# Whole tiles for half tiles, and sums of squared keys issued later, in the preparation of an RWKV-7 and attention encoder layer

## The chip, the cores and the metric

The kernel runs on one core of a Trainium2 chip. Times are device microseconds of one execution; the figure for a kernel is the median of several timed executions. The profile is of one further execution, taken by the hardware profiler, and its times run from the start of the span.

## The reference

One encoder layer over 512 tokens of width 1024, in float32. A normalised input is projected; the columns feed an RWKV-7 branch (8 heads of 64, two directions), a differential attention branch, and two gates. Cut to what the change touches:

```
k, r, v   = slices of centred_shift(rmsnorm(x) @ w_in)
kk        = k * k_k, per head divided by its norm: kk / sqrt(sum(kk * kk))
decay     = exp(-exp(w_log)),  a = sigmoid(...)             # per token and direction
k_dir     = k * (1 + (a - 1) * k_a)
# scan over the tokens, one per direction, state of 64 x 64 per head:
sa        = state @ (-kk_t)
state     = state * w_t + sa (x) (kk_t * a_t) + v_t (x) k_t
y_t       = state @ r_t
```

The kernel replaces the scan by eight chunks of 64 tokens. For each chunk it needs products of r, kk, k and a with running products of the decay, and the 64 x 64 matrices between them.

## The kernel before

**Stages.** The program first normalises and projects (lines 297 to 330), then comes the *preparation* (335 to 552), in which this change lies; after it the program reads back what the preparation wrote, inverts the triangular blocks on VectorE (`diag_blocks`) between the steps of the attention, and runs the chunks one after another, then the output projections and the feed-forward part.

**Precision.** Each dense product is three matmuls (`mm3`, lines 245 to 247): a high and a low half of the weights (`whi`, `wlo`, made by ScalarE in line 131 and VectorE in line 135 from `raw`) against a high and a low half of the activations. One projection of 128 columns is 24 matmuls.

**First half of the preparation.** `proj_in` makes the four key tiles: projections `in4` to `in7`, each emptied from PSUM by VectorE into the single buffer `un` (line 369) and shifted into `k` by ScalarE (370) and VectorE (371, 372). ScalarE squares each key tile into `ksq` (406). `key_sums(p)` (line 398) lets TensorE add these squares per head into the PSUM tile `nrm`: four small matmuls of 8 columns (two records each). It is called two projections later, and the last two are placed among the matmuls of the next dense product, `pp`, four tiles in each of two halves (`pp00`, `pp10` and on: the first digit is the tile, the second the half). `issue_after(last_mm.ins)` fixes the place of the sums on TensorE behind the last dense matmul that had been issued. ScalarE empties `pp` into the tile `pps` (432). When all sums are there, ScalarE and VectorE make the reciprocal norm, and TensorE turns it (`kin`, line 442).

**The loop.** For four head pairs p and two directions d (eight turns) the program makes: `sg`, `th` (ScalarE), the running sum `en` (VectorE, 478 or 480), its exponentials `ep` and `en` (ScalarE), `kd` (492), `ae` (494), the tile `bkt` by two products (500 and 499), and the tiles `ga`. A `ga` tile holds four chunks of 512 columns; there are two for each turn, h = 0 and 1. Columns 448 to 511 are r times `ep` (503), 385 to 447 are minus kk times the shifted `ep` (505 or 508), and column 384 is a copy on ScalarE (506 or 509). TensorE then multiplies `bkt` with these 128 columns (`aps`, 517), VectorE masks the result into columns 0 to 255 of the same tile (519), TensorE turns `bkt` (`xps`, 522) and ScalarE puts that into columns 256 to 383 (523). SyncE writes the tile to DRAM (`gad`, 525) and its diagonal blocks to another tensor (`md`, 528). The tag `ga` has four buffers of four chunks each, which `lr`, `pps` and these tiles take in turn; a buffer is written again when all that read it, DMAs too, have finished.

**Order.** Each engine works through its instructions in order. Within a stage a scheduler sets that order from the data and the places given; a changed instruction therefore moves others around it. TensorE's dense matmuls of later tiles (`in`, `da`) fill the time between the small ones.

Of the kernel before, what the change touches and what calls it, by code (L numbers as in the profile page):

```python
# [10 lines left out]
F32 = mybir.dt.float32  # L11
F32R = mybir.dt.float32r
AF = mybir.ActivationFunctionType
ALU = mybir.AluOpType
AX = mybir.AxisListType

P = 128
# [3 lines left out]
NCH = T // C  # L21
# [133 lines left out]
def tile_hybrid_encoder(ctx, tc, xT, wts, par, cst_a, cst_p, lor, lqk, nfin, out, dbg=None):  # L155
    nc = tc.nc
# [178 lines left out]
    pp = pool("prep", side="right")  # L335
    cp = pp.tile([P, CP["bk"]], F32, name="cp")
    nc.sync.dma_start(cp, cst_p[:, 0:CP["bk"]])
    lr = pp.tile([P, 2, 512], F32, tag="ga", name="lr", bufs=4)
    nc.sync.dma_start(lr, lor[:, 0:2, :])


# [53 lines left out]
    def key_sums(p):  # L395
        with tc.issue_after(last_mm.ins):
            for tt in range(4):
                nc.tensor.matmul(nrm[:, tt, :], sqs[p][:, tokens(tt)], cp[:, CP["selk"] + 8 * p:CP["selk"] + 8 * p + 8], start=(p == 0 and tt == 0), stop=(p == 3 and tt == 3))

    kt = []  # L400
    for p in range(4):
        k_ = tmp("k", f"k{p}", bufs=4)
        proj_in(4 + p, k_)
        kt.append(k_)
        sq = tmp(("sg", "th")[p % 2], f"ksq{p}", bufs=2)
        nc.scalar.activation(sq, k_, AF.Square, scale=par_col("kk", p))
        sqs[p] = sq
        if p > 1:
            key_sums(p - 2)
    for kind in range(2):  # L410
        for d in range(2):
            rows, other = lrows(kind, d)
# [7 lines left out]
    pTh, pTl = W.next("pT")  # L420
    for h in range(2):
        wh, wl = W.next("pp", h)
        pps = pp.tile([P, 4, 512], F32, tag="ga", name=f"pps{h}", bufs=4)
        for tt in range(4):
            ps = psd.tile([P, T], F32, tag="d", name=f"pp{tt}{h}") if tt % 2 == 0 else psm.tile([P, T], F32, tag="m", name=f"pp{tt}{h}")
            for k in range(2):
                tk = slice(k * T + tt * P, k * T + (tt + 1) * P)
                wk = slice(k * 512, (k + 1) * 512)
                last_mm = mm3(ps, pTh[:, tk], pTl[:, tk], wh[:, wk], wl[:, wk], k == 0, k == 1)
            if h == 0 and tt in (0, 2):  # L430
                key_sums(2 + tt // 2)
            nc.scalar.activation(pps[:, tt, :], ps, AF.Copy)
        nc.sync.dma_start(ppd[:, :, h * 512:(h + 1) * 512].rearrange("a q f -> q a f"), pps)

# [11 lines left out]
    for p in range(4):  # L446
# [17 lines left out]
        for d in range(2):  # L464
# [29 lines left out]
            nc.vector.scalar_tensor_tensor(ae, th, 1.0, en, ALU.add, ALU.mult)  # L494
            aec, kdc, rc = chunks(ae), chunks(kd), chunks(r_)
            bkt = pp.tile([P, NCH, P], F32, tag="bk", name=f"bk{p}{d}", bufs=2)
            ga = [pp.tile([P, 4, 512], F32, tag="ga", name=f"ga{p}{d}{h}", bufs=4) for h in range(2)]
            rv_ = slice(None, None, 1 if d == 0 else -1)
            nc.vector.scalar_tensor_tensor(bkt[:, :, 0:C][:, :, rv_], aec, 0.5, kkc, ALU.mult, ALU.mult)
            nc.vector.tensor_tensor(bkt[:, :, C:P], kdc, enc, ALU.mult)  # L500
            for h in range(2):
                hs = slice(4 * h, 4 * h + 4)
                nc.vector.tensor_tensor(ga[h][:, :, 448:512], rc[:, hs, :], epc[:, hs, :], ALU.mult)
                if d == 0:
                    nc.vector.scalar_tensor_tensor(ga[h][:, :, 385:448], kkc[:, hs, 1:], -1.0, epc[:, hs, 0:63], ALU.mult, ALU.mult)
                    nc.scalar.activation(ga[h][:, :, 384:385], kkc[:, hs, 0:1], AF.Copy, scale=-1.0)
                else:
                    nc.vector.scalar_tensor_tensor(ga[h][:, :, 385:448][:, :, ::-1], kkc[:, hs, 0:63], -1.0, epc[:, hs, 1:], ALU.mult, ALU.mult)
                    nc.scalar.activation(ga[h][:, :, 384:385], kkc[:, hs, 63:64], AF.Copy, scale=-1.0)
            mk = cp[:, CP[f"m{d}"]:CP[f"m{d}"] + P]  # L510
            for h in range(2):
                g_ = ga[h]
                aps = [psm.tile([P, 4, P], F32, tag="m", name=f"aps{p}{d}{h}{hh}") for hh in range(2)]
                for c in range(4):
                    for hh in range(2):
                        rows = slice(hh * 64, hh * 64 + 64)
                        nc.tensor.matmul(aps[hh][:, c, :], bkt[rows, 4 * h + c, :], g_[rows, c, 384:512], start=True, stop=True)
                for hh in range(2):
                    nc.vector.tensor_tensor(g_[:, :, P * hh:P * hh + P], aps[hh], mk[:, None, :].broadcast_to([P, 4, P]), ALU.mult)
                xps = psm.tile([P, 4, P], F32, tag="m", name=f"xps{p}{d}{h}")  # L520
                for c in range(4):
                    nc.tensor.transpose(xps[:, c, :], bkt[:, 4 * h + c, :], ident)
                nc.scalar.activation(g_[:, :, 256:384], xps, AF.Copy)
                cs = slice(d * NCH + 4 * h, d * NCH + 4 * h + 4)
                nc.sync.dma_start(gad[cs, :, p, :].rearrange("c q x -> q c x"), g_)
                mdv = md.rearrange("(x u) s t -> x u s t", u=8)
                for hh in range(2):
                    nc.sync.dma_start(mdv[cs, 2 * p + hh].rearrange("c s t -> s c t"), g_[0:64, :, P * hh:P * hh + 64])
# [956 lines left out]
```

## Time and profile before

| what | us |
|---|---|
| median of 3 timed runs | 937.24 |
| lowest and highest | 936.47, 937.66 |
| the profiled execution's own time | 939.69 |
| its span | 937.9 |
| TensorE busy in the span | 884.5 (94%) |
| VectorE busy | 570.4 (61%) |
| ScalarE busy | 431.0 (46%) |

The shares are means over stages with different limits, so they say little about this change. To read it, take the stretches of the preparation apart and look in each for the engine that the others wait for. A row of a timeline gives the start, the time of one instruction (or of several alike in a row, from the first's start to the last's end), and in brackets how long the engine had been idle and what ended that. Two operations in a row on one engine overlap, so what an operation costs its engine is the distance from its start to the next start.

### The profile page before, as it was taken

Reading aid. Unit: us, or ns where it says so; the run is one execution under the profiler, and the core shown is the slowest. Engines: PE = TensorE matmul, PEld = TensorE weight load, DVE = VectorE, ACT = ScalarE, POOL = GpSimd, SP = SyncE. Lnnn points to the kernel's source line nnn. Section 1 sums busy time; section 2 is a strip of 40 time slices with the busy share of each in tenths; the row PEclk is TensorE's granted clock in tenths of the full one; section 3 lists DMA queues with packets and bytes.
Section 4 is the critical chain, followed back from the end, with each engine's and each line's share of the span. In section 5 each row is a group of like instructions: output and inputs, shape, how many; then the busy total and the mean of one; then the engine's idle time right before and its main releaser. Section 6 shows DMA issues by size and latency. Waiting matters only on the chain.

```text
span 937.9 us, 14083 instructions
## 1 busy us (share of the span) xinstructions
PE 884.5 (94%) x5640; PEld 741.7 (79%) x5640; DVE 570.4 (61%) x873; ACT 431.0 (46%) x677; POOL 51.7 (6%) x74
## 2 busy tenths in 40 slices
PE   5899898999999996899999999999999999999995
PEld 3788777788567785788877888888888888888884
DVE  7756999769985521467897665554354445334453
ACT  6665555453577531332464544542153235213555
POOL 5000000010000012322000000000000000000000
PEclk9989999999899997899999999999999999999998
DMA  5534788795245258586125423232323232323502
GB/s 214 186 113 146 255 262 265 246 372 164 90 151 123 81 145 244 169 292 209 33 80 192 143 90 104 99 109 94 110 93 113 90 113 90 113 91 111 201 25 90
DMA packets 65553, 138.58 MB, mean 148 GB/s; under 512 B 25808, under 2 KB 28112, under 8 KB 63184
## 3 DMA queue, kind: packets, MB, share of 16 engines
q1 hardware_dynamic: 61248, 114.09, 37.3%
q0 software_dynamic: 4240, 23.60, 7.5%
q8 instruction: 44, 0.72, 0.3%
q14 instruction: 21, 0.17, 0.1%
HBM read 106.73 MB, written 30.93 MB: 147 GB/s over the span
## 4 chain that ended last, share of the span: by engine, by line
PE 65%; DVE 15%; ACT 8%; issue 5%; DMA 5%; SPq 1%; POOL 0%; POOLq 0%; DVEq 0%; ACTq 0%
PE f L246 12%; PE f L247 12%; PE f L245 12%; PE gA L655 4%; DVE wlo L135 2%; PE ss L1023 2%; PE yy L1023 2%; PE sc L655 2%; PE ov L655 1%; DMA md<-ga 1%; ACT whi L131 1%; DMA mi<-md 1%; PE wout L246 1%; DVE mi L580 1%; PE wout L247 1%
## 5 line engine op out<-in xcount | busy, mean ns | idle before, releaser
L131 ACT ACTIVATE whi<-raw 128x1024 fp32r<-128x1024 f32 x134 | 141.4, 1057 | 288.9 <-PE f L246 182.8
L135 DVE TENSOR_TENSOR wlo<-raw,whi 128x1024 fp32r<-128x1024 f32 x134 | 166.8, 1247 | 51.9 <-ACT whi L131 51.0
L247 PE MATMUL f<-fh,wlo 128*128 128x512 f32 x256 | 97.2, 380 | 0.0
L246 PE MATMUL f<-fl,whi 128*128 128x512 f32 x256 | 97.1, 379 | 0.0
L245 PE MATMUL f<-fh,whi 128*128 128x512 f32 x256 | 97.1, 379 | 0.0
L245 PE MATMUL f<-h1h,whi 128*128 128x512 f32 x256 | 97.0, 379 | 0.0
L246 PE MATMUL f<-h1l,whi 128*128 128x512 f32 x256 | 97.0, 379 | 0.0
L247 PE MATMUL f<-h1h,wlo 128*128 128x512 f32 x256 | 97.0, 379 | 0.0
L1262 DVE TENSOR_TENSOR x<-x,f 128x512 f32<-128x512 f32 x32 | 22.0, 687 | 89.5 <-PE f L247 89.5
L1251 DVE SCALAR_TENSOR_TENSOR ft<-f,rf 128x512 f32<-128x512 f32 x32 | 22.1, 691 | 63.5 <-PE f L247 63.4
L245 PE MATMUL in<-hhi,whi 128*128 128x512 f32 x128 | 51.0, 399 | 7.5 <-ACT whi L131 7.5
L246 PEld LDWEIGHTS f<-h1l,whi 128*128 128x128 f32 x256 | 48.4, 189 | 6.9
L245 PEld LDWEIGHTS f<-h1h,whi 128*128 128x128 f32 x256 | 48.4, 189 | 6.9
L247 PEld LDWEIGHTS f<-h1h,wlo 128*128 128x128 f32 x256 | 48.4, 189 | 6.9
L245 PEld LDWEIGHTS f<-fh,whi 128*128 128x128 f32 x256 | 48.4, 189 | 6.8
L247 PEld LDWEIGHTS f<-fh,wlo 128*128 128x128 f32 x256 | 48.4, 189 | 6.8
L246 PEld LDWEIGHTS f<-fl,whi 128*128 128x128 f32 x256 | 48.4, 189 | 6.8
L246 PE MATMUL in<-hlo,whi 128*128 128x512 f32 x128 | 50.9, 397 | 2.1 <-DVE hlo L301 2.1
L247 PE MATMUL in<-hhi,wlo 128*128 128x512 f32 x128 | 50.3, 393 | 1.1 <-DVE wlo L135 1.1
L245 PEld LDWEIGHTS in<-hhi,whi 128*128 128x128 f32 x128 | 25.3, 198 | 11.1 <-ACT whi L131 7.5
L246 PEld LDWEIGHTS in<-hlo,whi 128*128 128x128 f32 x128 | 25.3, 197 | 7.6 <-DVE hlo L301 4.3
L1254 DVE TENSOR_TENSOR h1l<-ft,h1h 128x512 fp32r<-128x512 f32 x32 | 25.7, 804 | 8.7 <-ACT h1h L1253 8.7
(362 smaller groups left out, 1840.0 us busy)
## 6 DMA issues: line engine op xcount, KB each, us to landing
raw<-in_wts_dram SPq DMA_DIRECT2D x134, 512.0 KB, 3.5
gad<-ga SPq DMA_DIRECT2D x16, 1024.0 KB, 5.6
sga<-gad POOLq DMA_DIRECT2D x16, 1024.0 KB, 7.7
xs<-in_xT_dram SPq DMA_DIRECT2D x8, 256.0 KB, 5.5
ppd<-pps SPq DMA_DIRECT2D x2, 1024.0 KB, 5.7
md<-ga SPq DMA_DIRECT2D x32, 64.0 KB, 4.9
gates<-go SPq DMA_DIRECT2D x8, 256.0 KB, 2.1
mi<-md POOLq DMA_DIRECT2D x1, 2048.0 KB, 12.7
```

Of the source, the lines that this page charges most:

```text
L131: a = nc.scalar.activation(hi, raw, AF.Copy)
L135: b = nc.vector.tensor_tensor(lo, raw, hi.bitcast(F32), ALU.subtract)
L245: nc.tensor.matmul(ps, lh, moved(rh), start=first, stop=False)
L246: nc.tensor.matmul(ps, lh, moved(rl), start=False, stop=False)
L247: return nc.tensor.matmul(ps, ll, moved(rh), start=False, stop=last)
L580: behind[e] = f(*args, **kw)
L655: last_pe = f(*args, **kw)
L1023: seq_last = nc.tensor.matmul(*args, **kw)
L1251: nc.vector.scalar_tensor_tensor(t_, ps, 0.0, rf, ALU.max, ALU.mult)
L1254: nc.vector.tensor_tensor(halves(hl_[:, f, :]), turns(t_), halves(hh_[:, f, :].bitcast(F32)), ALU.subtract)
L1262: nc.vector.tensor_tensor(x[:, f, :], x[:, f, :], ps, ALU.add)
```

## The change

Three things change, all in the preparation. The tag `ga` has two buffers of eight chunks for four of four, and each turn fills one such tile: the products in lines 503, 505 and 508 and ScalarE's copies in 506 and 509 are issued once over eight chunks, not twice over four. What follows works on halves of that tile, as before on the two tiles. And the key sums are issued one projection later: those of pair 0 behind the eighth projection, those of pairs 1, 2 and 3 behind the first, second and third tile of `pp`.

```
-    lr = pp.tile([P, 2, 512], F32, tag="ga", name="lr", bufs=4)
+    lr = pp.tile([P, 2, 512], F32, tag="ga", name="lr", bufs=2)
...
         sqs[p] = sq
-        if p > 1:
-            key_sums(p - 2)
+        if p > 2:
+            key_sums(p - 3)
...
-        pps = pp.tile([P, 4, 512], F32, tag="ga", name=f"pps{h}", bufs=4)
+        pps = pp.tile([P, 4, 512], F32, tag="ga", name=f"pps{h}", bufs=2)
...
-            if h == 0 and tt in (0, 2):
-                key_sums(2 + tt // 2)
+            if h == 0 and tt < 3:
+                key_sums(1 + tt)
...
-            ga = [pp.tile([P, 4, 512], F32, tag="ga", name=f"ga{p}{d}{h}", bufs=4) for h in range(2)]
+            ga = pp.tile([P, NCH, 512], F32, tag="ga", name=f"ga{p}{d}", bufs=2)
...
-            for h in range(2):
-                hs = slice(4 * h, 4 * h + 4)
-                nc.vector.tensor_tensor(ga[h][:, :, 448:512], rc[:, hs, :], epc[:, hs, :], ALU.mult)
-                if d == 0:
-                    nc.vector.scalar_tensor_tensor(ga[h][:, :, 385:448], kkc[:, hs, 1:], -1.0, epc[:, hs, 0:63], ALU.mult, ALU.mult)
-                    nc.scalar.activation(ga[h][:, :, 384:385], kkc[:, hs, 0:1], AF.Copy, scale=-1.0)
...
+            nc.vector.tensor_tensor(ga[:, :, 448:512], rc, epc, ALU.mult)
+            if d == 0:
+                nc.vector.scalar_tensor_tensor(ga[:, :, 385:448], kkc[:, :, 1:], -1.0, epc[:, :, 0:63], ALU.mult, ALU.mult)
+                nc.scalar.activation(ga[:, :, 384:385], kkc[:, :, 0:1], AF.Copy, scale=-1.0)
...
             for h in range(2):
-                g_ = ga[h]
+                g_ = ga[:, 4 * h:4 * h + 4]
```

On TensorE, at the end of the key projections, this stood before (numbers at the names are buffers; `in6`, `in7` are the projections of pairs 2 and 3, `ksq0` and `ksq1` the squares of pairs 0 and 1):

```order
L247 MATMUL in6_372<-hhi_79,wlo4_290 128x512
L398 MATMUL nrm_286<-cp_259,ksq0_324 128x8 x4
L245 MATMUL in7_415<-hhi_79,whi5_328 128x512
...
L247 MATMUL in7_415<-hhi_79,wlo5_329 128x512
L398 MATMUL nrm_286<-cp_259,ksq1_363 128x8 x4
L245 MATMUL pp10_496<-whi7_410,whi6_367 128x512
L246 MATMUL pp10_496<-wlo7_411,whi6_367 128x512
L245 MATMUL pp00_484<-whi7_410,whi6_367 128x512
```

And now:

```order
L247 MATMUL in6_372<-hhi_79,wlo4_290 128x512
L245 MATMUL in7_411<-hhi_79,whi5_328 128x512
...
L247 MATMUL in7_411<-hhi_79,wlo5_329 128x512
L398 MATMUL nrm_286<-cp_259,ksq0_324 128x8 x4
L245 MATMUL pp10_492<-whi7_406,whi6_367 128x512
L246 MATMUL pp10_492<-wlo7_407,whi6_367 128x512
L245 MATMUL pp00_480<-whi7_406,whi6_367 128x512
...
L247 MATMUL pp00_480<-whi7_406,wlo6_368 128x512
L398 MATMUL nrm_286<-cp_259,ksq1_363 128x8 x4
```

The sums of pair 0 have gone behind all 24 matmuls of `in7`, and those of pair 1 behind the six of `pp00`.

On VectorE, in the seventh turn (pair 3, direction 0; `ga300` and `ga301` are its two tiles), this stood before:

```order
L503 TENSOR_TENSOR ga300_1421<-r3_1311,ep30_1410 128x4x64
L505 SCALAR_TENSOR_TENSOR ga300_1421<-kkn3_1387,ep30_1410 128x4x63
L494 SCALAR_TENSOR_TENSOR ae30_1418<-th30_1405,en30_1408 128x512
L500 TENSOR_TENSOR bk30_1420<-kd30_1416,en30_1408 128x8x64
L499 SCALAR_TENSOR_TENSOR bk30_1420<-ae30_1418,kkn3_1387 128x8x64
L503 TENSOR_TENSOR ga301_1422<-r3_1311,ep30_1410 128x4x64
L505 SCALAR_TENSOR_TENSOR ga301_1422<-kkn3_1387,ep30_1410 128x4x63
L519 TENSOR_TENSOR ga300_1421<-aps3000_1431,cp_259 128x4x128
```

And now:

```order
L501 TENSOR_TENSOR ga30_1397<-r3_1287,ep30_1386 128x8x64
L503 SCALAR_TENSOR_TENSOR ga30_1397<-kkn3_1363,ep30_1386 128x8x63
L494 SCALAR_TENSOR_TENSOR ae30_1394<-th30_1381,en30_1384 128x512
L500 TENSOR_TENSOR bk30_1396<-kd30_1392,en30_1384 128x8x64
L499 SCALAR_TENSOR_TENSOR bk30_1396<-ae30_1394,kkn3_1363 128x8x64
L517 TENSOR_TENSOR ga30_1397<-aps3000_1403,cp_259 128x4x128
```

Both products over all eight chunks stand ahead of `ae` and `bk` now, and the masking (line 519 before, 517 now) follows `bk` at once.

## Rows read from the trace of the kernel before

**Rows 1.** Busy us by stretch: PE, PEld, DVE, ACT, POOL (instructions); PEclk, DMA share, GB/s.
```profile
55.00:68.60 13.60, 13.52 (x73) 11.58 (x72) 6.59 (x9) 9.86 (x16) 0.00 (x0) 1.00 0.41 126
88.00:184.00 96.00, 86.33 (x583) 69.51 (x582) 91.82 (x149) 53.88 (x105) 0.00 (x0) 1.00 0.73 239
```

**Rows 2.** Timeline of TensorE, 43 to 69 us: start, duration, instruction, idle before.
```profile
43.09 0.38 PE L247 MATMUL in<-hhi,wlo 128*128 128x512 f32 x1
45.45 1.65 PE L398 MATMUL nrm<-cp,ksq 128*128 128x8 f32 x8 [1.98 <-ACT ksq L406]
...
52.62 0.38 PE L246 MATMUL in<-hlo,whi 128*128 128x512 f32 x1
...
54.78 0.38 PE L247 MATMUL in<-hhi,wlo 128*128 128x512 f32 x1
54.99 1.00 PE L398 MATMUL nrm<-cp,ksq 128*128 128x8 f32 x8
55.85 0.46 PE L245 MATMUL pp<-whi,whi 128*128 128x512 f32 x1
...
56.36 0.38 PE L245 MATMUL pp<-whi,whi 128*128 128x512 f32 x1
...
68.61 0.60 PE L442 MATMUL kin<-ca,kinv 128*8 128x128 f32 x4
```

**Rows 3.** The same table by stretch, single microseconds around the slow clock.
```profile
45.00:46.00 1.00, 0.55 (x4) 0.55 (x4) 0.69 (x1) 0.98 (x2) 0.00 (x0) 0.88 0.00 0
46.00:47.00 1.00, 1.00 (x7) 1.00 (x6) 0.69 (x1) 0.98 (x2) 0.00 (x0) 0.50 0.00 0
...
52.00:53.00 1.00, 1.00 (x4) 0.81 (x4) 0.02 (x1) 0.00 (x0) 0.00 (x0) 0.71 0.00 0
```

**Rows 4.** Timelines of ScalarE and VectorE: what the key sums and `pp` wait for.
```profile
44.69 0.71 ACT L406 ACTIVATE ksq<-k,pr 128x512 f32<-128x512 f32 x1
50.67 0.72 ACT L406 ACTIVATE ksq<-k,pr 128x512 f32<-128x512 f32 x1 [1.49 <-DVE k L372]
27.26 1.22 DVE L135 TENSOR_TENSOR wlo<-raw,whi 128x1024 fp32r<-128x1024 f32 x1
51.33 0.69 DVE L369 TENSOR_TENSOR un<-in,rbs 128x512 f32<-128x512 f32 x1
```

**Rows 5.** Timeline of VectorE, seventh turn and the start of the eighth.
```profile
165.84 0.42 DVE L503 TENSOR_TENSOR ga<-r,ep 128x256 f32<-128x256 f32 x1
166.18 0.42 DVE L505 SCALAR_TENSOR_TENSOR ga<-kkn,ep 128x252 f32<-128x252 f32 x1
...
167.11 0.69 DVE L500 TENSOR_TENSOR bk<-kd,en 128x512 f32<-128x512 f32 x1
167.72 0.69 DVE L499 SCALAR_TENSOR_TENSOR bk<-ae,kkn 128x512 f32<-128x512 f32 x1
...
169.72 1.29 DVE L519 TENSOR_TENSOR ga<-aps,cp 128x512 f32<-128x512 f32 x2 [0.64 <-PE aps L517]
...
174.32 1.23 DVE L480 TENSOR_TENSOR_SCAN en<-cp,sg 128x512 f32<-128x512 f32 x1 [1.61 <-ACT sg L474]
```

**Rows 6.** Timeline of TensorE in the eighth turn, and the two microseconds behind.
```profile
178.95 1.16 PE L517 MATMUL aps<-ga,bk 64*128 64x128 f32 x16 [2.00 <-DVE bk L499]
178.00:180.00 2.00, 1.05 (x16) 1.00 (x16) 2.00 (x5) 0.00 (x0) 0.00 (x0) 1.00 0.49 126
```

**Rows 7.** Chain of waits behind the loop: start, duration, what.
```profile
186.05 4.90 DMA md<-ga
...
191.70 12.72 DMA mi<-md
```

**Rows 8.** SyncE's queue in the second turn, landing of the tiles, ScalarE in the third.
```profile
112.09 2.33 SPq L528 DMA_DIRECT2D md<-ga  x2
DMA to landing us min/median/max: 2.2/5.0/7.1
122.09 0.60 ACT L523 ACTIVATE ga<-xps 128x512 f32<-128x512 f32 x1 [1.08 <-PE xps L522]
```

More of the change, by code (lines that the diff above doesn't have):

```diff
@@ L500, in tile_hybrid_encoder @@
             nc.vector.tensor_tensor(bkt[:, :, C:P], kdc, enc, ALU.mult)
-            for h in range(2):
-                hs = slice(4 * h, 4 * h + 4)
-                nc.vector.tensor_tensor(ga[h][:, :, 448:512], rc[:, hs, :], epc[:, hs, :], ALU.mult)
-                if d == 0:
-                    nc.vector.scalar_tensor_tensor(ga[h][:, :, 385:448], kkc[:, hs, 1:], -1.0, epc[:, hs, 0:63], ALU.mult, ALU.mult)
-                    nc.scalar.activation(ga[h][:, :, 384:385], kkc[:, hs, 0:1], AF.Copy, scale=-1.0)
-                else:
-                    nc.vector.scalar_tensor_tensor(ga[h][:, :, 385:448][:, :, ::-1], kkc[:, hs, 0:63], -1.0, epc[:, hs, 1:], ALU.mult, ALU.mult)
-                    nc.scalar.activation(ga[h][:, :, 384:385], kkc[:, hs, 63:64], AF.Copy, scale=-1.0)
+            nc.vector.tensor_tensor(ga[:, :, 448:512], rc, epc, ALU.mult)
+            if d == 0:
+                nc.vector.scalar_tensor_tensor(ga[:, :, 385:448], kkc[:, :, 1:], -1.0, epc[:, :, 0:63], ALU.mult, ALU.mult)
+                nc.scalar.activation(ga[:, :, 384:385], kkc[:, :, 0:1], AF.Copy, scale=-1.0)
+            else:
+                nc.vector.scalar_tensor_tensor(ga[:, :, 385:448][:, :, ::-1], kkc[:, :, 0:63], -1.0, epc[:, :, 1:], ALU.mult, ALU.mult)
+                nc.scalar.activation(ga[:, :, 384:385], kkc[:, :, 63:64], AF.Copy, scale=-1.0)
             mk = cp[:, CP[f"m{d}"]:CP[f"m{d}"] + P]
             for h in range(2):
-                g_ = ga[h]
+                g_ = ga[:, 4 * h:4 * h + 4]
                 aps = [psm.tile([P, 4, P], F32, tag="m", name=f"aps{p}{d}{h}{hh}") for hh in range(2)]
```

## The prediction

> **What bounds the kernel now.** I read the busy time by stretch first, then TensorE's timeline at the start of the preparation, then VectorE's timeline in the loop behind it, and last the chain of waits. The table by stretch [rows 1] shows two regimes. From 55 to 68.6 us TensorE is busy 13.52 of 13.6 us: the second half of this part is paced by matmuls. From 88 to 184 us, the loop over four head pairs and two directions (eight turns), VectorE is busy 91.82 of 96 us and TensorE 86.33: VectorE paces it, and TensorE waits for it.
>
> Before the first regime TensorE has a hole. Its last matmul of `in6` starts at 43.09, and the next thing in its queue, the sums over the squared keys of pair 0 (`nrm`), starts only at 45.45, because ScalarE writes those squares from 44.69 to 45.40 [rows 2, 4]. Then the clock falls: the granted clock is 0.88 in the microsecond 45 to 46, 0.50 in the next, and 0.71 in the one from 52 to 53 [rows 3]. With the level 1.2 GHz at 0.50 and 2.4 GHz at 1.00, that is a slow stretch from 45.76 (0.24 us of that microsecond at half) to 52.42 (0.58 us at half): 6.7 us, of which half, 3.3 us, is lost.
>
> Whatever moves the end of the loop moves the end of the kernel. In the chain of waits the last diagonal blocks are written to DRAM (`md`, 186.05, 4.90 us), read back (`mi`, 191.70, 12.72 us) [rows 7], and VectorE starts on them when they have landed; nothing in this stretch waits on another clock. I carry a shift of the loop's end one to one to the end of the kernel. Against that shift stand only changes in where the later, lower granted clocks fall, which I put at 1 us either way by the size of the 3.3 us above and by the three timed runs, 1.2 us apart.
>
> **The key sums, three products later.** What moves is four `nrm` operations on TensorE; nothing is added or removed. Step by step, from rows 2 and 4:
> The eighth projection `in7` no longer stands behind `nrm` of pair 0. Its weights were split by 28.5 us (27.26 plus 1.22), so it starts right behind `in6`, at 43.3.
> It has 24 matmuls. At the full clock they come 0.216 us apart (52.62 to 54.78 is ten steps), so `in7` ends at 43.3 + 5.2 = 48.5. Before it ended at 54.99.
> Now `nrm` of pair 0, 0.86 us (54.99 to 55.85): to 49.35. Its squares are there since 45.40, so this wait is gone.
> Two matmuls of `pp10`, 0.51 us (55.85 to 56.36): to 49.9.
> What is late next is the accumulator of `pp00`. It is the PSUM buffer that `in6` filled, and VectorE empties it with `un` from 51.33 to 52.02, behind work that has nothing to do with the moved sums. Thus TensorE stands from 49.9 to 52.05, 2.15 us, where before it stood 2.0 us at 45.45. The hole is moved, not closed.
> Behind `pp00` before: 56.36 to the transposes `kin` at 68.61 is 12.25 us. After, one more `nrm` (pair 1) stands in that piece: 12.25 + 0.86 = 13.1. At the full clock `kin` comes at 52.05 + 13.1 = 65.15.
>
> Against 68.61 that is 3.45 us earlier. But 3.3 us of the 68.61 are the slow clock: without it the old order would have come out at 65.3. The order itself is worth 0.15 us, and the rest hangs on the clock after the new hole. Bounds from rows of this case: after the hole at 43.3, with 1.65 us of tiny `nrm` work behind it, the clock fell; after a hole of 2.00 us ahead of 178.95 it did not, the granted clock being 1.00 in the two microseconds that follow [rows 6]. In the new place 0.86 us of `nrm` and 0.51 us of matmuls lie ahead of a hole of 2.15 us, 3.5 us in all with hardly any wide matmul in it, much as before from 43.3 to 47.1 (45.45 + 1.65). That is nearer to the first row. I take: it falls again, for about as long, and the term is -0.15 us; the ends are -3.45 (no fall) and +3.15 (a slow stretch twice as long, below).
>
> Do the other readers follow? The squares of pair 1 are written from 50.67 to 51.4, ahead of their new place. Those of pairs 2 and 3 come earlier with `in7`: the weight buffer that it frees, and with it the next split on ScalarE and VectorE and all that is queued behind, comes free at 48.5 for 54.99. I find no new wait there at the full clock.
>
> **One tile of eight chunks.** Per turn VectorE issues two products of 512 (504) elements in place of four of 256 (252), and ScalarE one copy for two. Lengths of operations overlap, so what counts is the distance from start to start: 0.34 us for 256 elements (165.84 to 166.18), 0.61 for 512 (167.11 to 167.72) [rows 5]. A pair of small ones costs 0.67, the large one 0.60: 0.067 us less, 16 pairs, 1.07 us of VectorE in the whole loop. ScalarE's eight fewer copies are worth nothing: it waits for TensorE in each turn, as the 1.08 us ahead of 122.09 [rows 8].
>
> The price is in the order. Before, only the first half's two products (0.67 us) stood ahead of `ae` and the two `bk` products, and the second half's came behind. Now both whole products (1.20 us) stand ahead of `bk` in most turns, and TensorE's `aps` wait for `bk`. So `aps` starts 0.53 us later within a turn. Where VectorE has other work between `bk` and the masking of `aps` that hides it; this holds in the first six turns, which have projections and weight splits there. In the last two it has none: VectorE already waits 0.64 us for `aps` at 169.72 and 1.61 us for ScalarE's `sg` at 174.32 [rows 5], so the cover is gone and the delay is paid. Sum: six turns at 2 x 0.067 = 0.134, -0.80; seventh turn +0.53; eighth, where only the sums of `kd` stand between, an estimate of +0.38 between nothing and 0.53, nearer to the latter. Together +0.1 us. The ends are -1.07 (all saved) and +1.06 (two turns at +0.53, nothing saved).
>
> The Trainium skill (Perfetto Trace Analysis, Optimizing Scalar/DVE Operations) says two things here that pull apart: each VectorE operation carries some 60 ns, so grouping pays when that engine is saturated; and where an engine is not saturated but makes others wait, breaking operations up lets work be done sooner. By the first alone the loop would gain 16 x 60 ns, an estimate of 1.0 us; by the second alone the last two turns lose. The trace agrees with both, with 67 ns and with the waits of 0.64 and 1.61 us.
>
> **Buffers.** The pool keeps its size, two whole tiles for four halves. A whole tile can be written again only when all six transfers of the turn two before have landed. Tightest is the fourth turn: the last transfers of the second are issued by 112.09 + 2.33 = 114.4, and with the longest landing, 7.1 us, are there at 121.5 [rows 8]. ScalarE's copy into the new tile stands in its queue at 120.4, with the emptying of `xps` behind it. A delay of 1.1 us there fits into the 1.08 us it waits ahead of 122.09 anyway. I cost this at 0; the bound is some 1 us in one turn.
>
> **Sum.** Profiled execution: 939.69 us, a span of 937.9 with 1.8 around it, 2.45 above the median of the timed runs, 937.24. The terms, -0.15 and +0.1, give 939.6 for such an execution and 937.2 against the median.
>
> **Rivals.**
> A, the clock holds. For it: the row at 178.95, and that the hole lies between wide matmuls. Against: the same 3.5 us of little work as before. It gives -3.45 + 0.1: 933.9.
> B, slower: the clock falls at the new hole and stays low. For it: behind the new hole come three `nrm` within one product each, and at the low clock one takes 1.65 us (the row at 45.45), so the wide work between them is broken up, where `in7` was 24 wide matmuls in one piece. Price: a second stretch like that of 6.7 us, 3.3 us more. From the point at which the clock is still at half when the second of these sums starts, near 60 us, it decides. 937.2 + 3.3 = 940.5. Against it: TensorE has no further hole there.
> C, the loop gains all of its 1.07 us because the waits of the last turns are hidden by reordering: 937.24 - 0.15 - 1.07 = 936.0.
> D, the whole tile waits for its transfers in every turn, or the change does less than it says: about +1 us in two or three turns, 939.5.
>
> **How the numbers follow.** Forecast 0.36, A 0.33, B 0.18, C 0.08, D 0.05. A measurement of this kernel tells 0.2%, 1.9 us, from no change: 935.4 to 939.1. Faster: nearly all of A (0.31), a ninth of the forecast by the later clocks (0.04), a quarter of C (0.02): 0.37. Slower: B 0.18, most of D 0.04, of the forecast 0.04: 0.26. The rest, 0.37, is no change. The range reaches from A less 0.9 to just past B, 933.0 to 940.6, so that half of B and the outer part of A, some 0.15 in all, are left out; the forecast's own range is 935.6 to 938.8.
>
> **What would show it.** TensorE: no idle ahead of the first `nrm`, `in7` from 43.3 to 48.5, a wait of 2.1 us for VectorE's `un` ahead of `pp00` at 52. The granted clock between 50 and 68 us decides between forecast, A and B, as does the start of `kin`: 68.5, 65.2 or 71.7. VectorE: eight products of each kind at about 0.68 us; a longer wait for `aps` in the seventh turn, 1.1 to 1.2 us for 0.64. The last `md` transfer then stands within 0.6 us of the shift of `kin`. The forecast is wrong if the hole is not there at all, if the clock holds, or if the shift of `kin` does not reach `mi`.

## The result and the profile after

| | before | after |
|---|---|---|
| median of 6 timed executions, us | 937.45 | 943.62 |
| lowest and highest | 936.47, 939.11 | 940.58, 947.72 |
| the profiled execution's own time | 939.69 | 940.58 |
| its span | 937.9 | 938.8 |

The change makes the kernel slower: ratio 1.0065, 95% interval 1.0041 to 1.0090, some 6.2 us. The prediction was no change, 937.2, and its range ended at 940.6. Ratios here and below leave out disturbed executions of either kernel, medians don't. The profiled execution of after is the shortest of its six, so its span shows 0.9 us of the loss. To see the rest, the span is cut at points that both kernels have, and each piece is compared (e1 and e8 are experiments, told below).

| piece of the profiled execution, us | before | after | after less before | e1 | e8 |
|---|---|---|---|---|---|
| start to the first `un` (VectorE) | 30.12 | 29.44 | -0.68 | 29.32 | 29.71 |
| to `kin` (TensorE) | 38.49 | 38.01 | -0.48 | 37.36 | 37.07 |
| to the scan of the first turn | 19.47 | 19.47 | 0 | 19.47 | 19.47 |
| to the scan of the eighth turn | 86.24 | 87.42 | +1.18 | 87.44 | 87.44 |
| to the last `bv` (VectorE) | 8.95 | 12.24 | +3.29 | 12.15 | 9.48 |
| to the issue of `mi` (GpSimd) | 8.43 | 5.86 | -2.57 | 5.79 | 7.51 |
| to VectorE's first operation on `mi` | 12.74 | 18.73 | +5.99 | 10.81 | 11.01 |
| to VectorE's first weighing of `e` | 36.93 | 37.03 | +0.10 | 38.17 | 36.92 |
| to the end | 696.53 | 690.60 | -5.93 | 693.09 | 695.19 |

The first piece lies ahead of all that was changed; over the 17 profiled executions of this study it takes between 29.3 and 32.1 us. The two large pieces cancel in this one execution. The last goes with the granted clock, which differs from execution to execution: over the 17 it takes between 689.6 and 696.8 us, the longer the more of it ran at the lower clock (a correlation of 0.89; that the clock is the whole of it is not shown), and the kernels with the change don't stand apart from those without it. Before has the first pair of these rows (240 to 262 and 360 to 400 us; the clock is the third number from the right), after the second pair:

```profile
240.00:262.00 22.00, 20.18 (x74) 11.23 (x72) 19.89 (x41) 14.90 (x34) 0.00 (x0) 0.84 0.29 96
360.00:400.00 40.00, 28.59 (x427) 23.92 (x425) 13.95 (x27) 9.55 (x22) 12.04 (x21) 0.79 0.73 222
```

```profile
240.00:262.00 22.00, 20.72 (x86) 12.92 (x85) 19.91 (x36) 11.70 (x25) 0.00 (x0) 1.00 0.29 95
360.00:400.00 40.00, 28.65 (x387) 24.14 (x387) 12.60 (x25) 9.75 (x22) 13.53 (x23) 0.87 0.73 224
```

What after loses in its other executions is then to be looked for ahead of it, and there stand 5.99 us in one wait. VectorE's queue after the loop, in after:

```profile
208.04 0.36 DVE L595 TENSOR_TENSOR lq<-lq 128x64 f32<-128x64 f32 x2 [10.02 <-DMA lq<-in_lqk_dram]
...
208.57 1.22 DVE L135 TENSOR_TENSOR wlo<-raw,whi 128x1024 fp32r<-128x1024 f32 x1
...
211.17 0.22 DVE L578 TENSOR_TENSOR tmpo<-mi 128x60 f32<-128x60 f32 x1
```

`lq` is a load of 128 KB (line 594 before, 592 after) from which the attention makes one scalar. VectorE waits 10 us for it, and behind it in the same queue stand a weight split, the rotation of keys, and the whole work on `mi`. `mi` itself had landed at 203.74 (issued 192.44, 11.3 us), so it waited 7.4 us for a scalar that is first read at 247.9. Before, VectorE took `mi` when it landed (first operation 204.44). TensorE stands behind the split:

```profile
204.51 0.38 PE L245 MATMUL da<-whi,hhi 128*128 128x512 f32 x1
209.84 0.80 PE L246 MATMUL da<-wlo,hhi 128*128 128x512 f32 x1 [4.95 <-DVE wlo L135]
```

Why is `lq` late? SyncE issues it behind two weight loads, GpSimd issues `mi`. Before, then after (SyncE's queue, GpSimd's, and the line of `lq` on the landing):

```profile
189.44 2.09 SPq L127 DMA_DIRECT2D raw<-in_wts_dram  x2
191.62 0.38 SPq L594 DMA_DIRECT2D lq<-in_lqk_dram  x1
...
191.70 0.70 POOL L614 DMA_DIRECT2D mi<-md  x1 [166.40 <-DMA bvd<-bv]
...
DMA to landing us min/median/max: 5.1/5.1/5.1
```

```profile
191.51 2.92 SPq L127 DMA_DIRECT2D raw<-in_wts_dram  x2
194.53 0.44 SPq L592 DMA_DIRECT2D lq<-in_lqk_dram  x1
...
192.44 0.70 POOL L612 DMA_DIRECT2D mi<-md  x1 [167.83 <-DMA bvd<-bv]
...
DMA to landing us min/median/max: 13.5/13.5/13.5
```

Before, `lq` is issued 0.08 us ahead of `mi`, after 2.09 us behind it. The transfers of each queue show what that means. In after, for 194 to 196, 196 to 198 and 200 to 204 us (queue, packets, MB, share of the time of 16 engines; the software queue is GpSimd's, the hardware queue SyncE's):

```profile
q0 software_dynamic: 20, 0.33, 66.7%
q1 hardware_dynamic: 50, 0.14, 17.3%
...
q0 software_dynamic: 42, 0.69, 88.1%
q1 hardware_dynamic: 2, 0.01, 1.0%
...
q0 software_dynamic: 141, 1.20, 71.8%
q1 hardware_dynamic: 138, 0.41, 25.6%
```

The first packets of GpSimd's loads (`mi`, 2 MB, and four of 1 MB behind it) move between 194 and 196 us, some 2 us after the issue of `mi`. From then on SyncE's queue gets next to nothing for some 2 us (2 packets of 44 from 196 to 198) and a quarter of the time afterwards. What SyncE issued early enough has landed by then; what it issued later waits for the large loads. The Trainium skill (DMA: Bandwidth & Descriptors, Queues, rings and completion order) states that each engine goes round the queues packet by packet, where a packet is typically several descriptors. If the profile counted the same packets, the trace would agree from 200 to 204 us, 141 against 138, and not from 196 to 198, 42 against 2; no run here shows whether it counts the same.

The clock and the hole at the end of the loop answer to [rows 6]; in after (TensorE, then single stretches of three microseconds, columns as in rows 1):

```profile
179.50 2.08 PE L515 MATMUL aps<-ga,bk 64*128 64x128 f32 x16 [3.61 <-DVE bk L499]
```

```profile
180.00:183.00 3.00, 3.00 (x24) 2.45 (x23) 2.03 (x3) 0.33 (x1) 0.00 (x0) 0.50 0.00 0
183.00:186.00 3.00, 3.00 (x23) 2.54 (x21) 1.29 (x2) 0.54 (x2) 0.00 (x0) 0.57 0.72 253
```

The hole ahead of `aps` is 3.61 us, where it was 2.00; 14 dense matmuls stand between `za` and `aps` in this turn now, not 19; and the clock falls to its lower level (0.50, 1.2 GHz), so that `aps` takes 2.08 us for 1.16. That delays the dense matmuls behind it, the weight splits that wait for these, the weight loads that wait for the splits, and `lq` behind the second of these loads. The split in question, before and after; it ends 0.45 us ahead of the issue of `lq` in both:

```profile
189.94 1.23 DVE L135 TENSOR_TENSOR wlo<-raw,whi 128x1024 fp32r<-128x1024 f32 x1 [1.37 <-ACT whi L131]
```

```profile
192.85 1.23 DVE L135 TENSOR_TENSOR wlo<-raw,whi 128x1024 fp32r<-128x1024 f32 x1 [1.36 <-ACT whi L131]
```

### The profile page after: what moved, and what is told of

Same layout as the page of the kernel before. It is cut to its first block, busy times and chain, and to the rows that moved or that the text cites. A ratio compares the mean times of both kernels' runs of the same rounds, so it can differ in the third digit from the quotient of the medians.

```text
span 938.8 us, 14058 instructions
## 1 busy us (share of the span) xinstructions
PE 878.9 (94%) x5640; PEld 739.0 (79%) x5640; DVE 570.9 (61%) x857; ACT 429.9 (46%) x669; POOL 51.7 (6%) x74
## 4 chain that ended last, share of the span: by engine, by line
PE 68%; DVE 13%; ACT 7%; issue 5%; DMA 5%; POOL 0%; SPq 0%; DVEq 0%; POOLq 0%; ACTq 0%
PE f L246 12%; PE f L247 12%; PE f L245 12%; PE gA L653 4%; DVE wlo L135 3%; PE ss L1021 2%; PE yy L1021 2%; PE sc L653 2%; PE ov L653 1%; ACT whi L131 1%; DMA lq<-in_lqk_dram 1%; PE wout L246 1%; PE wout L247 1%; PE wout L245 1%; PE al L1021 1%
## 6 DMA issues: line engine op xcount, KB each, us to landing
mi<-md POOLq DMA_DIRECT2D x1, 2048.0 KB, 11.3
```

## The experiments

The first runs set two theories against each other. A: the loss is `lq` landing late. B: the loss is the loop's later end, carried on. A ratio is to the kernel before, run on the same chip in the same rounds; the last two columns are in us and from the one profiled execution (a minus sign: ahead of `mi`). A filler is one or more matmuls whose result nobody reads.

| kernel | ratio, 95% interval | `lq` issued, from `mi` | `lq` landed after |
|---|---|---|---|
| e9 after, `lq` ahead on SyncE | 0.9996 (0.9972, 1.0021) | -2.63 | 2.9 us |
| e15 before, filler | 0.9987 (0.9963, 1.0011) | -0.32 | 3.8 |
| before | 1 | -0.08 | 5.1 |
| e13 key sums alone, filler | 0.9998 (0.9975, 1.0022) | -0.02 | 4.7 |
| e14 after, filler | 1.0024 (0.9991, 1.0058) | +0.06 | 8.9 |
| e4 whole tile alone | 1.0060 (1.0033, 1.0087) | +1.02 | 14.9 |
| e3 key sums alone | 1.0057 (1.0032, 1.0082) | +1.56 | 13.8 |
| after | 1.0065 (1.0041, 1.0090) | +2.09 | 13.5 |
| e2 before, `lq` late | 1.0045 (1.0022, 1.0069) | +3.80 | 15.0 |
| e1 after, `lq` on GpSimd | 1.0000 (0.9979, 1.0021) | -19.1 | 4.4 |
| e5 before, the same | 0.9991 (0.9960, 1.0021) | -18.7 | 4.0 |
| e6 key sums alone, the same | 0.9988 (0.9956, 1.0021) | -18.5 | 3.7 |
| e7 whole tile alone, the same | 0.9985 (0.9961, 1.0009) | -19.1 | 3.8 |
| e8 e1 with a filler | 0.9994 (0.9969, 1.0019) | -18.2 | 4.2 |
| e12 e1 with four products | 1.0008 (0.9978, 1.0037) | -18.5 | 3.7 |
| e10 e1 with two fillers | 0.9973 (0.9943, 1.0003) | -18.2 | 6.8 |
| e11 before, `lq` on GpSimd, two fillers | 0.9972 (0.9944, 1.0000) | -18.4 | 4.5 |

**e1: `lq` out of the way, nothing else.**

```
-    nc.sync.dma_start(lq, lqk)
+    nc.gpsimd.dma_start(lq, lqk)
```

> The kernel after the change, with one line other: the small load lq (128 KB) is issued by GpSimd, right ahead of its load mi, and no longer by SyncE behind two weight loads. TensorE's order stays as it is. Theory A (the small load lq, issued 2.1 us behind mi, lands after 13.5 us, and VectorE's and then TensorE's queue stand behind it): lq lands in about 5 us, VectorE's wait of 10.0 us goes, the first operation on mi starts near 204 us as before the change (211.2 after it), TensorE's hole of 4.95 us at 204.9 is gone; time 937 us, between 935.5 and 939. Theory B (the loop's end, 2.7 us later by the slow clock in the eighth turn, is what is carried to the end, and the rest is the later clock): 942 to 944, no difference to after.

Measured: 936.71 against 936.13 of before, ratio 1.0000. The loss is gone, as far as an interval of 0.2% each way tells, though the eighth turn is as slow as in after (`aps` 2.08 us, hole 3.61). VectorE waits for `mi` alone:

```profile
195.97 0.35 DVE L595 TENSOR_TENSOR lq<-lq 128x64 f32<-128x64 f32 x2
...
202.34 0.22 DVE L578 TENSOR_TENSOR tmpo<-mi 128x60 f32<-128x60 f32 x1 [2.04 <-DMA mi<-md]
```

Theory B fails: the late loop end is still there, and the lost time isn't. A part of what the earlier start on `mi` gives goes again in the next piece (38.17 for 36.93); from the issue of `mi` to the first weighing of `e` it is 49.67 us before, 55.76 in after and 48.98 in e1.

**e2: the kernel before, with only `lq` late.** The load and what is made from it are written behind the second list of weights.

```
-    nc.sync.dma_start(lq, lqk)
...
     wqkv = [W.next("intok", 1920 + 512, k2) for k2 in range(4)]
+    with tc.issue_after(W.sent.ins):
+        nc.sync.dma_start(lq, lqk)
```

> The kernel before the change, with lq issued by SyncE one weight load later (some 194 us, 2.3 us behind mi), and what is computed from it written as much later. Nothing of the change is in it: TensorE's order and the eighth turn are those of before. Theory A: lq lands after 13 us at 207 to 208, VectorE's first operation on mi moves from 204.4 to about 209, 4.5 us, and the kernel takes 940 to 943. No hole on TensorE, since no weight split stands behind lq here. Theory B: 937.4, no difference, since the loop ends where it did.

Measured: 939.83 for 936.13, ratio 1.0045. A late `lq` alone, with none of the change, costs some 4.2 us by the ratio. In its profiled execution the clock fell in the eighth turn too, though no line of that turn was touched (8.95 us became 10.51); e6, e7 and e9, told below, show that this alone is no loss that can be told. One part of the expectation was wrong: a weight split does stand behind the delayed work on `mi`, and TensorE waits 6.71 us for it at 224.58.

```profile
210.40 0.36 DVE L825 TENSOR_TENSOR lq<-lq 128x64 f32<-128x64 f32 x2 [11.47 <-DMA lq<-in_lqk_dram]
```

**e3 and e4: each part of the change alone.** e3 keeps the half tiles of before and moves the key sums; e4 keeps the key sums and takes the whole tile. Their diffs are the two halves of the change.

> Only the key sums are moved; half tiles in four buffers as before the change. Theory A: the loop starts about 1.2 us earlier, its last turn has 19 dense matmuls ahead of aps as before, so no slow clock there, lq stays ahead of mi or within a few tenths of it; 936.2, between 935 and 938. Rival (the moved sums cost the time, by the clock that falls at the new hole or by the order behind it): 941 to 944.

> Only the whole tile; key sums as before the change. TensorE has 14 dense matmuls, not 19, ahead of aps in the eighth turn, as in the kernel after. Theory A: hole of some 3.6 us there, slow clock, loop's last mask 2.7 to 3.9 us later than before, lq issued behind mi and landing after 13 us; 943 to 945. Rival (the time is the moved sums'): 937 to 938, by the two products of the last turns +0.1.

Measured: e3 942.00, e4 942.87, against 936.13. Each part alone costs nearly all of the loss, so they don't add. The expectation for e3 was wrong: its eighth turn has the hole of 2.00 us of before, and yet the clock fell there, 0.62 from 180 to 183 us, and `lq` was late:

```profile
180.00:183.00 3.00, 3.00 (x26) 2.45 (x28) 2.96 (x6) 0.60 (x1) 0.00 (x0) 0.62 0.00 1
```

```profile
194.12 0.38 SPq L594 DMA_DIRECT2D lq<-in_lqk_dram  x1
```

**e5, e6, e7: `lq` out of the way in the other three.** The one line of e1, in before, e3 and e4.

> The kernel before the change, with the small load lq issued by GpSimd ahead of mi, as in e1. Theory A, as it stands after the first four runs (lq behind mi by 1.0 to 3.8 us landed after 13.5 to 15.0 us in each of e2, e3, e4 and after; in the profiled execution of before it was 0.08 us ahead of mi and landed in 5.1): in most executions of before lq is ahead anyway, so little changes, 934.5 to 936.5 against 936.1. If it were behind in half of them, 933.5. Rival (the place of lq matters by its slot in SyncE's queue, where the weight loads now start earlier): a gain of 2 us or more.

> Key sums moved, half tiles, and lq issued by GpSimd ahead of mi. Theory A: all that the moved sums cost in e3 (5.4 us) came through lq landing late, behind a slow clock in the eighth turn; with lq out of the way 935.5 to 937.5, level with before. Rival (the sums have a cost of their own at the start, by the clock behind the new hole at 50 to 56 us): 939 to 942.

> Whole tile, key sums as before, and lq issued by GpSimd ahead of mi. Theory A: as e6, 935 to 937.5. Rival (the whole tile's own cost in the last turns, 2.7 us of slow clock carried to mi): 938 to 941.

Measured: 935.32, 936.37, 935.46, with 938.20 for before in these rounds; ratios 0.9991, 0.9988, 0.9985. With e1 that makes four kernels, with and without each part of the change, that can't be told from before, nor, by their intervals, from each other. What can be told of the cost of either part (some 0.3% at best) comes through `lq`.

**e8: no hole in the eighth turn.** e1 and two matmuls that nobody reads:

```
+            if (p, d) == (3, 1):
+                fil = psm.tile([P, T], F32, tag="so", name="fil", bufs=1)
+                for _ in range(2):
+                    nc.tensor.matmul(fil, cp[:, CP["blk"]:CP["blk"] + P], ga[:, :, 448:512], start=True, stop=True)
```

> The kernel of e1, and two wide float32 matmuls more in the eighth turn (1 us each, on a spare PSUM bank, their result is not used), which read the first product over the whole tile: they stand on TensorE between the last dense matmul and aps, in the hole of 3.6 us. If the slow clock at the end of the loop comes from that hole: granted clock 1.00 from 177 to 186 us, aps 1.16 us for 2.08, the last mask of the loop ends some 2.5 us earlier, and, since mi is then issued earlier, 934 to 936 against 936.7 of e1. Rival (the slow clock has another cause, or mi waits for something else): aps 2.08 again, or no gain, 936.5 to 937.5.

Measured: 936.20, ratio 0.9994, no gain over e1 that can be told. The clock did what was expected:

```profile
178.84 1.16 PE L519 MATMUL aps<-ga,bk 64*128 64x128 f32 x16 [0.51 <-DVE bk L499]
```

```profile
180.00:183.00 3.00, 3.00 (x28) 2.23 (x28) 2.58 (x5) 1.19 (x2) 0.00 (x0) 1.00 0.27 85
```

The last `bv` comes 2.67 us earlier in its turn than in e1 (9.48 for 12.15), and `mi` only 0.95 us (16.99 behind the eighth scan for 17.94): SyncE's queue of `gad` and `md` stands between them. In these two executions most of what the slow clock costs at the end of the loop is hidden, with `lq` out of its way.

**e9: the moment or the queue?** In e1 `lq` changed both.

```
+    lq = keep.tile([P, 4, C], F32, name="lq")
...
-        nc.sync.dma_start(bvd[p], bv)
+        sent_bv = nc.sync.dma_start(bvd[p], bv)
...
+    with tc.issue_after(sent_bv.ins):
+        nc.sync.dma_start(lq, lqk)
     proj_in(14, sgd)
...
-    lq = at.tile([P, 4, C], F32, tag="lq", name="lq", bufs=1)
...
-    nc.sync.dma_start(lq, lqk)
```

> The kernel after the change, with lq issued by SyncE as before, but right behind the last bvd and ahead of the weight loads (into a tile of its own, so that it need not wait for the preparation's tiles). TensorE's order is that of after. It tells the moment from the queue: in e1 lq went through another engine's queue and 19 us ahead of mi. Theory A (what counts is that lq is issued ahead of mi): lq some 2.5 us ahead of mi, lands in 3 to 6 us, VectorE does not wait for it, no hole on TensorE at 205; 935.5 to 938. Rival (loads from SyncE's queue are served behind GpSimd's large loads whatever their moment, e1 gained by the route): lq lands after more than 10 us, 941 to 944.

Measured: 935.99, ratio 0.9996. On SyncE's own queue, but 2.63 us ahead of `mi`, `lq` lands in 2.9 us. It is the moment.

```profile
189.93 0.40 SPq L538 DMA_DIRECT2D lq<-in_lqk_dram  x1
...
192.56 0.70 POOL L613 DMA_DIRECT2D mi<-md  x1 [167.20 <-DMA lq<-in_lqk_dram]
```

**e10 and e11: both holes filled.** e10 is e8 with twelve wide matmuls behind the first key sums; e11 is e5 with eight ahead of them and one float32 matmul in the eighth turn.

```
+    def wide(n, name):
+        fil = psm.tile([P, T], F32, tag="m", name=name)
+        with tc.issue_after(last_mm.ins):
+            for _ in range(n):
+                nc.tensor.matmul(fil, hhi[:, 0, 0:P], moved(hhi[:, 0, :]), start=True, stop=True)
```

> The kernel of e8 (lq by GpSimd, two float32 matmuls in the hole of the eighth turn) and twelve wide matmuls more, on a spare PSUM bank with an unused result, behind the first key sums, in the hole ahead of pp00 (some 49 to 52.5 us). It tests the prediction's first term, that the rest hangs on the clock after the new hole. If so: granted clock 1.00 from 46 to 66 us, kin at about 65.3 (67.5 in after), loop start 1.5 to 3 us earlier than in e1 and e8 (86.2), and if a shift of the loop reaches the end, 933 to 935. Rival (a shift at the start is eaten in the loop by waits for ScalarE's sg and TensorE's aps): 936 as e8.

> The kernel before the change with lq issued by GpSimd as in e5, eight wide matmuls more between in6 and the first key sums (the hole of 2 us at 43.3), and one float32 matmul of 512 columns in the hole of the eighth turn; their results are not used. If the clock falls in these two places because of the holes: 1.00 from 42 to 66 us, loop start at 85 to 86 us (88.1 in before), aps of the eighth turn at 1.16 us each; 932.5 to 935. Rival (the clock falls there all the same, or the shift does not reach the end): 935 to 937.

Measured: 933.96 and 935.08, with 936.35 for before; ratios 0.9973 and 0.9972, whose intervals reach 1.0003 and 1.0000. They are the lowest of the study and below after, but against before they lie at the edge of what can be told. The clock held in both; e11:

```profile
42.00:66.00 24.00, 22.38 (x118) 19.34 (x117) 15.52 (x21) 18.12 (x26) 0.00 (x0) 1.00 0.30 101
```

From the first `un` to `kin`, e11 needs 36.40 us where before needed 38.49 and e5 38.38. e10 needs 37.70 at the full clock, no less than e1 (37.36) and e8 (37.07) with a slow stretch. That does not say that the clock is worth nothing in the order of after, since e10 carries more: its fillers, and a wait of 0.96 us of ScalarE for a load of constants (`braw`) that e8 doesn't have. e14, told below, has the order of after without fillers in this place, and there the clock held by itself in its profiled execution:

```profile
42.00:50.00 8.00, 8.00 (x41) 7.04 (x39) 7.10 (x10) 7.80 (x12) 0.00 (x0) 1.00 0.18 66
50.00:60.00 10.00, 8.20 (x48) 7.09 (x48) 7.70 (x11) 5.54 (x9) 0.00 (x0) 1.00 0.33 107
60.00:70.00 10.00, 9.97 (x52) 8.41 (x52) 4.40 (x6) 8.17 (x12) 0.00 (x0) 1.00 0.58 164
```

It needs 35.47 us, 3.02 less than before; e4, with the old order and the full clock, 35.18.

**e12: merging or buffers?** e1 with the four products of before, into the whole tile.

> The kernel of e1 (after, lq by GpSimd), but with the products of decay in four operations over four chunks, as before the change, into the whole tile: only the buffers differ from e6. It tells the merging from the buffers. If the merging lengthens the hole ahead of aps in the eighth turn (both whole products ahead of bk, and fewer dense matmuls in between): hole back to 2.0 us, 19 dense matmuls, aps of the first half 0.5 us earlier relative to the scan; loop end (last mask) 8.9 us behind the scan where the clock holds, up to 10.5 where it falls, against 10.4 to 11.6 in e1 and after. The time hardly tells them: 935 to 937.5. If the buffers of two whole tiles matter: waits of ScalarE for md of 2 us and more, and the loop's start to end 1 us longer than the 95.2 us of before.

Measured: 937.64, ratio 1.0008. The hole is back to 2.00 us with 19 dense matmuls, and the eighth turn takes 8.95 us, as in before. From the first scan to the eighth it needs 86.54 us, where e6, with four buffers, needs 86.23 and e1, with merged products, 87.44. So the two large buffers cost 0.3 us (all of it in the seventh turn, 10.85 for 10.51), and the merging 0.9 us in seven turns and 0.53 in the eighth at the full clock (9.48 of e8 less 8.95).

```profile
179.18 1.16 PE L517 MATMUL aps<-ga,bk 64*128 64x128 f32 x16 [2.00 <-DVE bk L499]
```

**e13, e14, e15: how does each part make `lq` late?** With `lq` as in the kernels before and after, only the hole in the eighth turn is filled: by one matmul on `ae` in e13 (e3) and e15 (before), by the two of e8 in e14 (after).

> Only the key sums moved, as in e3, lq as before the change, and one float32 matmul of 512 columns more in the hole of 2 us ahead of aps in the eighth turn (its result is not used). If in e3 it was the slow clock of the eighth turn (0.62 from 180 to 183 us) that pushed lq behind mi: aps 1.16 us, lq within 0.2 us of mi or ahead of it, landing in 5 us, and 935 to 938. Rival (the moved sums make lq late without that clock): 940 to 943 as e3.

> The kernel after the change, lq as in it, with the two float32 matmuls of e8 in the hole of the eighth turn. Theory C (five dense matmuls fewer stand ahead of aps, 14 for 19, and must be done behind the loop, so that the second weight split, and lq behind it, come later even at the full clock): from e8, lq at 191.1 us against mi at 190.7, 0.4 us behind; if that is enough, lq lands after 13 us and the kernel takes 940 to 943. Rival (only the slow clock makes lq late, as in e3): lq lands in 5 us, 935.5 to 938.

> The kernel before the change with the same one float32 matmul in the eighth turn as e13, lq as it was. It is the control of e13 and asks whether the kernel before loses the race for lq in some of its executions: then a gain of 1 to 2 us, 934.5 to 935.5 for 936.3; if it never does, 936 to 937.

Measured: 937.09, 938.85 and 936.14, with 936.97 for before. In e13 the loss of e3 is gone (0.9998 for 1.0057): with the key sums alone it was the slow clock of the eighth turn that put `lq` behind `mi`. In e14 much of it seems gone (1.0024 for 1.0065, though the intervals overlap), and four of its twelve executions took over 943 us, as two of 29 did of before. In the profiled one `lq` and `mi` are issued almost at the same moment, and `lq` lands after 8.9 us:

```profile
199.50 0.36 DVE L599 TENSOR_TENSOR lq<-lq 128x64 f32<-128x64 f32 x2 [5.44 <-DMA lq<-in_lqk_dram]
```

With the hole filled, the lead of `lq` goes from 0.32 us (e15) over 0.02 (e13) to -0.06 (e14). That fits theory C, that the whole tile takes away some of the lead by its order alone (the five dense matmuls and the later `bk`), by less than it said, and that the slow clock takes the rest; but it rests on one execution each, and the interval of e14 holds both 1 and most of the loss, so how the whole tile's part divides is not shown. e15 shows that before loses nothing that can be told to this race.

**Left open.** Whether the clock falls in the eighth turn more often with the key sums moved, and why. With a hole of 2.00 us it fell in three profiled executions (e2, e3, e6) and held in three (before, e5, e12); with 3.61 us it fell in all five (after, e1, e4, e7, e9); with a filler in none of six. Six executions don't say how often. That it differs is suggested by the times, not shown: e3 loses what e13 doesn't, while before loses nothing that can be told against e15 (e3 and the other two ran on different chips, each beside before).

## Why the prediction was wrong, point by point

**The step that failed** is "Whatever moves the end of the loop moves the end of the kernel", with "I carry a shift of the loop's end one to one". It is wrong twice. The end of the loop (last `bv`) moved by 4.0 us in all within the preparation (-0.48 + 1.18 + 3.29), and the issue of `mi` by only 1.4, since SyncE's queue gave 2.57 back; and then 5.99 us came from a load that isn't on the chain of [rows 7] at all. e1 shows both: the eighth turn is as long there (12.15 us to the last `bv`), and no loss is left. The chain had `mi` at 191.70. What it doesn't show is that 0.08 us ahead of it another queue issued a load for which VectorE's queue would stop. The prediction named SyncE's queue in the buffers' step alone, and never asked what stands in it behind the loop. Its own sign of being wrong came: `kin` came 1.16 us earlier and the issue of `mi` 0.74 us later. The term for the later clocks, 1 us either way, was too small as well: the last piece of the table above differs by 5.93 us between these two executions.

**The key sums**: the order came as foreseen. Answering to [rows 2], in after:

```profile
47.80 1.00 PE L398 MATMUL nrm<-cp,ksq 128*128 128x8 f32 x8
...
52.75 0.80 PE L245 MATMUL pp<-whi,whi 128*128 128x512 f32 x1 [3.42 <-DVE un L369]
...
67.45 0.60 PE L442 MATMUL kin<-ca,kinv 128*8 128x128 f32 x4
```

`in7` runs straight on, no wait ahead of the sums, and the hole is moved, not closed: 3.42 us for the 2.15 forecast. 0.94 us of the difference fits a wait of ScalarE for the load `braw` at 36.95, which before didn't have in its profiled execution, and behind which its next weight split, VectorE's half of it and then `un` come as much later. The clock fell again, as the forecast took it, for half as long: answering to [rows 3],

```profile
52.00:53.00 1.00, 0.25 (x1) 0.25 (x2) 0.69 (x1) 1.00 (x3) 0.00 (x0) 0.72 0.04 12
...
55.00:56.00 1.00, 1.00 (x6) 0.87 (x4) 0.97 (x2) 0.29 (x1) 0.00 (x0) 0.57 0.68 119
```

The term was -0.15 and measured -0.48 (from the first `un`), inside its bounds, but as a sum of other parts: the clock gave back 1.7 us (1.7 lost for 3.4), the wait for `braw` took 0.94, and the order itself some 0.3, where 0.15 was to be gained (35.47 in e14 for 35.18 in e4, both at the full clock). That the sum came out near the forecast is luck. The slow stretch of before was also added up 0.08 us short: 0.58 us from 52.00 end at 52.58, so 3.4 us were lost and the order was worth 0.05 by the prediction's own rows. In other executions with the moved sums the same piece is -3.02 (e14), -1.13 (e1), +0.26 (e3) and +0.58 (e12) against before. Of the nine with that order and no filler in this place, the clock fell in eight and held in e14.

**The whole tile**: the term was +0.1, with +1.06 as its end, and measured +1.7 at the full clock (1.18 + 0.53, of which 0.3 belongs to the buffers, below); with the slow clock of the eighth turn, which the term didn't have, it was +4.5 in the profiled execution. The step "this holds in the first six turns, which have projections and weight splits there" failed. The scans of the eight turns in after, whose distances are the turns' lengths:

```profile
86.92 1.23 DVE L478 TENSOR_TENSOR_SCAN en<-cp,sg 128x512 f32<-128x512 f32 x1 [0.87 <-ACT sg L474]
99.55 1.22 DVE L480 TENSOR_TENSOR_SCAN en<-cp,sg 128x512 f32<-128x512 f32 x1
112.64 1.22 DVE L478 TENSOR_TENSOR_SCAN en<-cp,sg 128x512 f32<-128x512 f32 x1
123.57 1.22 DVE L480 TENSOR_TENSOR_SCAN en<-cp,sg 128x512 f32<-128x512 f32 x1 [0.46 <-ACT sg L474]
137.09 1.22 DVE L478 TENSOR_TENSOR_SCAN en<-cp,sg 128x512 f32<-128x512 f32 x1 [0.54 <-ACT sg L474]
148.61 1.23 DVE L480 TENSOR_TENSOR_SCAN en<-cp,sg 128x512 f32<-128x512 f32 x1 [0.31 <-ACT sg L474]
163.41 1.23 DVE L478 TENSOR_TENSOR_SCAN en<-cp,sg 128x512 f32<-128x512 f32 x1 [0.43 <-ACT sg L474]
174.34 1.23 DVE L480 TENSOR_TENSOR_SCAN en<-cp,sg 128x512 f32<-128x512 f32 x1 [1.60 <-ACT sg L474]
```

Before, they start at 88.08, 100.85, 114.00, 124.51, 137.66, 148.86, 163.80 and 174.32, so the seven turns differ by -0.14, -0.06, +0.42, +0.37, +0.32, -0.14 and +0.41. Where the cover holds in full, the saving is the 0.134 that was worked out (first and sixth turn). In the third and fourth VectorE now waits for `sg` at the end, 0.46 and 0.54 us, where before it didn't wait; the fifth has taken over an `un` from the sixth. e12, with four products, has the lengths of before in all six, so the merging does it. In the seventh the wait for `aps` grew from 0.64 to 1.31 us, near the 1.1 to 1.2 foreseen, but half of that comes with the buffers: it is 0.98 in e12. The delay of 0.53 that was worked out for `aps` is what the eighth turn pays at the full clock, where +0.38 was put. Of the rule from the Trainium skill (Perfetto Trace Analysis, Optimizing Scalar/DVE Operations) that the prediction weighed, breaking operations up was the half that held here: merged products cost 1.4 us in the loop (e12).

**The buffers**: costed at 0 with a bound of 1 us, they cost 0.3 (e12 against e6). The place was wrong: not the fourth turn but ScalarE's copies for the sixth and eighth tiles, which stand early in its queue and wait 2.16 and 2.06 us for `md` (in e12 only the eighth's waits, 1.39 us):

```profile
143.34 0.22 ACT L507 ACTIVATE ga<-kkn 128x8 f32<-128x8 f32 x1 [2.16 <-DMA md<-ga]
168.51 0.22 ACT L507 ACTIVATE ga<-kkn 128x8 f32<-128x8 f32 x1 [2.06 <-DMA md<-ga]
```

**The rivals**: A had its price about right: where the clock held in the new order (e14), the piece was 3.02 us shorter, for 3.45. Its condition didn't come true in after. B, the slower side, had the wrong place. Its mechanism, a hole on TensorE and a low clock behind it, did occur, but in the eighth turn, whose row [rows 6] was read as a sign that the clock can hold after 2 us of hole. That was one execution; in three others with the same hole it fell. That five dense matmuls had left this turn was in the order of the instructions and was not weighed. At the new hole itself the lower clock never cost more than the 3.4 us of before (e3, e6 and e12). C fell with the four turns that lose, D with the 0.3 us of the buffers.

## What to carry to other kernels

Beside the chain of waits, look in each queue for what is issued within a microsecond of a large transfer, and for who stops on it: a small load that leads a large one by 0.08 us is a cliff, not a slope, and any earlier change can push it over. Such a load belongs where its moment doesn't depend on the loop (one line in e1, a few in e9). When two changes each cost as much alone as together, look for a threshold behind both.

## What the runs showed of the hardware that was not expected

A load of 128 KB takes 2.9 to 5.1 us when issued up to 2.6 us ahead of the 2 MB load, 8.9 us at +0.06, and 13.5 to 15.0 us from 1.0 us behind it on. While the first packets of the large load move, the other queue almost stands: 2 packets against 42 in the two microseconds from 196 to 198 in after, 10 against 40 in before. And the same hole of 2.00 us on TensorE was followed by the lower clock in three of six executions, so one profile doesn't tell whether a hole costs its clock.
